# Query transposes for two heads at a time, their low parts written in the next unit, and later casts of the key weights in an encoder layer

## The chip, the cores and the metric

The kernel runs on one core of a Trainium2 chip. The metric is the device time of one execution in microseconds (us); a profile of one execution shows each engine's instructions: TensorE (PE for matmuls, PEld for the weight loads ahead of them), VectorE (DVE), ScalarE (ACT), GpSimd (POOL) and SyncE (SP), which issues most transfers.

## The reference

One encoder layer is computed for two sequences of 512 tokens and 1024 features (`x_prompt` and `x_sample`), in fp32:

```
h = rms_norm(x, ln1);  q, k, v, u, g_att, g_ssm = split(h @ w_in)
q = rms_norm(q per head of 64, q_gain);  k = rms_norm(k per head of 64, k_gain)
y_att = windowed_attention(q, k, v, sink, bias, mask)   # 16 heads, 4 key heads, blocks of 128, each block sees itself and its neighbours
y_ssm = s5_branch(u, ...)                               # bidirectional state-space scan, gelu, gated
x = x + (sigmoid(g_att) * y_att + sigmoid(g_ssm) * y_ssm) @ w_out
return x + square(relu(rms_norm(x, ln2) @ w_up)) @ w_down
```

In the attention each query block of 128 tokens meets up to three key blocks; the scores get a relative bias and a mask, a learned sink logit joins the softmax, and the weights multiply the values.

## The kernel before

Matmuls run on fp32 values split in two: a high part rounded to the engine's reduced fp32 form (F32R) and a low part, the difference between the value and its high part. A product is made of three matmuls (high by high, high by low, low by high) or, where both parts of one operand fill the two halves of the 128 partitions, of two.

The order of the work is written out by hand for TensorE, ScalarE and VectorE in the parts that the change touches (in the attention part for GpSimd too). Each engine runs its instructions in that order and stops at the first that waits. The transfers that SP issues are placed by the scheduler.

**The read-out** of the state-space branch comes first. It goes through 32 groups q of two channel groups: `turn_states` copies the states of the group after (L845 on ScalarE, or L847 on VectorE, and L848 on VectorE), `read_out` makes matmuls (L858, L860) into one of two PSUM buffers `sps`, `gelu` reads that buffer (L868 on ScalarE) and so frees it for the group after the next. Between these stand 28 items of other matmul work: 12 of the last two gates (L141) and then 16 of the keys' projection with the weights `w_k`. The weights come in pieces: `Block.piece` has SP load 512 KB into one of two buffers `c_raw` (L717), ScalarE cast it to the high part (L718), and returns the difference for the low part, which VectorE makes at the end of the group (L719). The dictionary `casts` names the group in which each piece is taken. In a group the casts stand ahead of the group's `gelu` on ScalarE. `last_cast` is the same for the last gate weights (L219, L220).

**The attention part** follows. It has 8 steps (a key head j of four query heads, and a sequence), each of four units (a query block qb of 128 tokens). Inside a unit the work of three things is interleaved:

- `Unit`, the attention of the query block: `scores(h)` for four heads (two matmuls each, L1048, stationary the query tile, moving the keys' high and low parts), `largest(h)` (L1052 on VectorE, which adds the bias and finds the negated maximum as a minimum; its second instruction reads the accumulator), `exp(h)` (L1058 on ScalarE).
- The unit before it (`prev`): `turn(i)` transposes the weights (L1064), `high(i)` and `low(i)` split them (L1068 on ScalarE, L1073 on VectorE), `value(i, part)` multiplies the values (L1080), `lower_part` copies half of the result (L1084 on ScalarE, tile `ol`) and `add` sums the halves (L1090, two instructions on VectorE). `add` runs in the unit after that.
- `Tile`, the queries of the next step: `project` (24 matmuls, L724), `square` (L1001 on ScalarE, tile `sq`), and a unit later, as `rows`: `power` (L1005 on VectorE, L1007 and L1008 on GpSimd), `norm`, `turn`, `high` and `low`.

The queries take this form. `norm` writes the normed tile (128 tokens by four heads of 64) to the first half of `qn`, and GpSimd copies it to the second, so that each head stands there twice:

```
self.qn = ap.tile([P, G, 2, HD], F32, tag="qn", name="qn")
V.tensor_mul(self.qn[:, :, 0], self.psv, self.rq[...])          # L1012
GP.tensor_copy(self.qn[:, :, 1], self.qn[:, :, 0])              # L1013
```

`turn` transposes each head with its double (four transposes, L1018), so that a head's 64 features lie in partitions 0 to 63 and again in 64 to 127. `high` writes the rounded, scaled value to all 128 partitions (one ScalarE instruction, L1023), and `low` overwrites partitions 64 to 127 with the difference (one VectorE instruction, L1027). The keys lie in both halves of the partitions too (`key_copies`, `key_turn`), so that one matmul against a query tile sums high and low part.

In a unit the order on VectorE around the change is: first minimum, `power`, `add`, second minimum, `prev.low(0)`, `norm`, third minimum, and so on; `rows.low` closes the unit. On TensorE `prev.value(0, 1)` needs `prev.low(0)`, and everything behind it follows in order. `acc` buffers (three in PSUM) hold the projections and the transposed queries.

Of the kernel before, what the change touches and what calls it, by code (L numbers as in the profile page):

```python
# [11 lines left out]
F32 = mybir.dt.float32  # L12
F32R = mybir.dt.float32r
I32 = mybir.dt.int32
AF = mybir.ActivationFunctionType
ALU = mybir.AluOpType
AX = mybir.AxisListType

P = 128
# [10 lines left out]
G = 4  # L30
HD = 64
# [32 lines left out]
def hybrid_layer(ctx, tc, x, xT, rel, onehot, early, w_qkv, w_ug, q_gain, k_gain, sink,  # L64
# [102 lines left out]
    def slot(pool):  # L167
        return [pool.tile([P, KT, HALF], F32R, tag=f"act{i}", name=f"act{i}") for i in range(2)]
# [603 lines left out]
    with tc.tile_pool(name="ssmo", bufs=2, reuse_waits="tile") as sp:  # L772
# [133 lines left out]
        casts = {0: [last_cast], 1: [last_cast], 2: [lambda: w_k.piece(0)], 3: [lambda: w_k.piece(1)], 8: [lambda: w_k.piece(2)], 9: [lambda: w_k.piece(3)],  # L906
# [46 lines left out]
    with tc.tile_pool(name="att", bufs=2, reuse_waits="tile") as ap:  # L953
# [32 lines left out]
        class Tile:  # L986
# [23 lines left out]
            def norm(self):  # L1010
                self.qn = ap.tile([P, G, 2, HD], F32, tag="qn", name="qn")
                V.tensor_mul(self.qn[:, :, 0], self.psv, self.rq[:, :, None].to_broadcast([P, G, HD]))  # L1012
                GP.tensor_copy(self.qn[:, :, 1], self.qn[:, :, 0])  # L1013

            def turn(self):
                self.pt = acc()
                for h in range(G):
                    PE.transpose(self.pt[:, h * P:(h + 1) * P], self.qn[:, h].rearrange("p a d -> p (a d)"), ident)  # L1018

            def high(self):  # L1020
                self.ptv = self.pt.rearrange("p (h t) -> p h t", h=G)
                self.dst = queries[self.key][:, :, self.t * P:(self.t + 1) * P]
                S.activation(self.dst, self.ptv, AF.Copy, scale=gain_q)  # L1023

            def low(self):
                dst = self.dst[64:128]
                V.scalar_tensor_tensor(dst, self.ptv[64:128], gain_q[64:128], dst.bitcast(F32),  # L1027
                                       op0=ALU.mult, op1=ALU.subtract)
# [164 lines left out]
        prev = owed = lower = None  # L1193
# [5 lines left out]
        if True:  # L1199
            rows = entry()  # L1200
            for i, (j, sq) in enumerate(steps):
# [8 lines left out]
                for qb in range(NB):  # L1210
# [21 lines left out]
                    cur.largest(1)  # L1232
                    if n3:
                        prev.turn(0)
                        prev.high(0)
# [56 lines left out]
                    if rows:  # L1292
                        if not sooner:
                            rows.high()
                        rows.low()
# [25 lines left out]
                if i == len(steps) - 2:  # L1321
# [3 lines left out]
                    y_tiles = [[[t_[:, 0:4, :], t_[:, 4:8, :]] for t_ in slot(slot_a)], split_slot()]  # L1325
            ahead = Column(1)
# [733 lines left out]
```

## Time and profile before

| what | value |
|---|---|
| time, median of 3 runs | 1470.08 us (1469.82 to 1471.71) |
| time of the profiled execution | 1469.22 us |
| span of the profiled execution | 1467.4 us |
| TensorE matmul busy | 1446.3 us, 99% |
| VectorE busy | 1094.6 us, 75% |
| ScalarE busy | 764.2 us, 52% |
| GpSimd busy | 168.9 us, 12% |
| granted TensorE clock | 0.999 |

The span is the time from the first to the last instruction of the profiled execution; the execution's own time is 1.8 us longer. In a row of the timeline stand the start, the duration, the engine, the line of the kernel, the operation, the tiles (written from read), the shapes, and in brackets the idle time before it and what ended it. In a row of a group stand the count, the busy time, the mean duration in ns and the idle time before. Busy time of TensorE counts matmuls whose ends are modelled and which overlap, so a wait shows first as a gap between starts.

### The profile page before, as it was taken

How to read it: one execution, taken by the hardware profiler on the slowest of the kernel's cores; microseconds unless marked ns; L12 is line 12 of the kernel's file. 1: busy time of each engine (PE TensorE's matmuls, PEld its weight loads, DVE VectorE, ACT ScalarE, POOL GpSimd, SP SyncE). 2: the span in 40 equal slices, each digit the busy share in tenths (PEclk: the TensorE clock that was granted, in tenths of full speed). 3: DMA queues.
4: the chain of work that ended last, by engine and by line, in shares of the span. 5: the costliest groups of instructions: out<-in, count | busy, mean ns of one | idle time of the engine just before them, and what ended most of it. 6: DMA issues, size and time to landing. Idle time of an engine off the chain costs nothing.

```text
span 1467.4 us, 21580 instructions
## 1 busy us (share of the span) xinstructions
PE 1446.3 (99%) x7782; PEld 1234.1 (84%) x7782; DVE 1094.6 (75%) x1836; ACT 764.2 (52%) x1366; POOL 168.9 (12%) x270
## 2 busy tenths in 40 slices
PE   6999999999999999999999999999999999999998
PEld 5888888888999899987888888888888888888887
DVE  7799979975636889888974689877776588575653
ACT  5489862233426778787532355554554444333332
POOL 4111120000223333343101000000000000000000
PEclk9999999999999999999999999999999999999999
DMA  8355567259941413236964134544443894454441
GB/s 300 112 171 174 161 206 268 101 178 290 307 131 35 121 46 89 95 130 217 303 212 144 72 115 165 174 149 147 155 158 123 302 346 147 158 177 153 129 129 58
DMA packets 129239, 243.86 MB, mean 166 GB/s; under 512 B 16060, under 2 KB 59324, under 8 KB 129133
## 3 DMA queue, kind: packets, MB, share of 16 engines
q1 hardware_dynamic: 104684, 186.87, 40.4%
q10 hardware_dynamic: 21888, 46.15, 8.3%
q0 software_dynamic: 2560, 9.48, 2.0%
q8 instruction: 61, 1.00, 0.3%
q14 instruction: 46, 0.37, 0.1%
HBM read 173.20 MB, written 81.82 MB: 174 GB/s over the span
## 4 chain that ended last, share of the span: by engine, by line
PE 91%; DVE 3%; ACT 2%; DMA 1%; issue 1%; POOL 1%; SPq 0%; DVEq 0%; ACTq 0%; POOLq 0%
PE bank L115 14%; PE bank L116 14%; PE bank L117 14%; PE acc L141 11%; PE acc L724 8%; PE acc L753 5%; PE acc L115 3%; PE acc L117 3%; PE acc L116 3%; PE po L1080 2%; PE sps L604 2%; PE sps L1048 2%; PE sps L860 2%; PE tps L1064 2%; PE lag L619 1%
## 5 line engine op out<-in xcount | busy, mean ns | idle before, releaser
L116 PE MATMUL bank<-b_lo,a_hi 128*128 128x512 f32 x440 | 171.2, 389 | 0.0
L117 PE MATMUL bank<-b_hi,a_lo 128*128 128x512 f32 x440 | 171.2, 389 | 0.0
L115 PE MATMUL bank<-b_hi,a_hi 128*128 128x512 f32 x440 | 171.2, 389 | 0.0
L724 PE MATMUL acc<-w_hi,hT 128*128 128x256 f32 x768 | 165.0, 291 | 0.0
L141 PE MATMUL acc<-hT,c_hi 128*128 128x512 f32 x512 | 161.1, 394 | 0.0
L1933 ACT CAST a_hi<-d_a 128x1024 fp32r<-128x1024 f32 x55 | 58.0, 1054 | 178.1 <-PE bank L116 175.2
L1934 DVE TENSOR_TENSOR a_lo<-d_a,a_hi 128x1024 fp32r<-128x1024 f32 x55 | 67.3, 1223 | 99.4 <-ACT a_hi L1933 97.3
L724 PEld LDWEIGHTS acc<-w_hi,hT 128*128 128x128 f32 x768 | 126.7, 190 | 1.7
L141 PEld LDWEIGHTS acc<-hT,c_hi 128*128 128x128 f32 x512 | 94.6, 188 | 21.0 <-issue 2.5
L724 PE MATMUL acc<-w_lo,hT 128*128 128x256 f32 x384 | 108.2, 282 | 0.0
L141 PE MATMUL acc<-hT,c_lo 128*128 128x512 f32 x256 | 100.3, 392 | 0.0
L115 PE MATMUL bank<-act,u_hi 128*128 128x512 f32 x256 | 99.6, 389 | 0.0
L116 PE MATMUL bank<-act,u_hi 128*128 128x512 f32 x256 | 99.6, 389 | 0.0
L117 PE MATMUL bank<-act,u_lo 128*128 128x512 f32 x256 | 99.6, 389 | 0.0
L117 PEld LDWEIGHTS bank<-b_hi,a_lo 128*128 128x128 f32 x440 | 82.6, 188 | 17.3
L115 PEld LDWEIGHTS bank<-b_hi,a_hi 128*128 128x128 f32 x440 | 82.6, 188 | 17.1
L116 PEld LDWEIGHTS bank<-b_lo,a_hi 128*128 128x128 f32 x440 | 82.6, 188 | 17.1
L1058 ACT ACTIVATE p<-p,nmx 128x257 f32<-128x257 f32 (+1 forms) x128 | 72.1, 564 | 27.0 <-DVE nmx L1052 24.3
L724 PEld LDWEIGHTS acc<-w_lo,hT 128*128 128x128 f32 x384 | 73.0, 190 | 2.5
L1052 DVE CUSTOM_DVE_ANT_0 p<-sps,bias,nsink 128x256 f32<-128x256 f32 (+1 forms) x128 | 69.2, 541 | 2.9 <-PE sps L1048 0.4
L1717 ACT CAST u_hi<-s 128x512 fp32r<-128x512 f32 x64 | 39.3, 621 | 59.8 <-PE bank L116 43.1
L1934 DVE TENSOR_TENSOR b_lo<-k,b_hi 128x1024 fp32r<-128x1024 f32 x55 | 66.9, 1217 | 0.0
(387 smaller groups left out, 3622.9 us busy)
## 6 DMA issues: line engine op xcount, KB each, us to landing
d_a<-a_scr SPq DMA_DIRECT2D x55, 512.0 KB, 3.6
u_raw<-in_w_up_dram SPq DMA_DIRECT2D x32, 512.0 KB, 5.7
a_scr<-t ACTq DMA_DIRECT2D x64, 256.0 KB, 2.1
k<-in_w_down_dram SPq DMA_DIRECT2D x32, 512.0 KB, 5.7
a_scr<-a ACTq DMA_DIRECT2D x48, 256.0 KB, 3.3
c_raw<-in_w_ug_dram SPq DMA_DIRECT2D x44, 256.0 KB, 3.6
ct_scr<-ctab SPq DMA_DIRECT2D x16, 576.0 KB, 3.3
ctab_in<-ct_scr SPq DMA_DIRECT2D x32, 288.0 KB, 4.7
```

The costliest lines, as they stand in the source:

```text
L115: PE.matmul(ps, a[0], b[0], start=first, stop=False)
L116: PE.matmul(ps, a[0], b[1], start=False, stop=False)
L117: PE.matmul(ps, a[1], b[0], start=False, stop=last)
L141: PE.matmul(self.ps[s], self.w[p == 2][:, k, :], hT[s][p == 1][:, k, :], start=i % (3 * KT) == 0, stop=i % (3 * KT) == 3 * KT - 1)
L604: PE.matmul(ps[:, i * P:(i + 1) * P], bm[:, ri, g, :], u_sb[:, g, :], start=True, stop=True)
L724: PE.matmul(ps, act[p == 2][:, k, col:col + P], self.w[k // 4][p == 1][:, k % 4, :], start=i == 0, stop=i == 3 * KT - 1)
L753: PE.matmul(self.ps[s], w_g[self.m][p == 2][:, k, :], y_part(s, int(p == 1), k), start=k + p == 0, stop=k == KT - 1 and p == 2)
L1052: V.tensor_tensor_reduce(self.p[:, h, 1:1 + self.nk], self.s[h][:, 0:self.nk], biases[self.j][h][:, b0:b0 + self.nk], -1.0, nsink[:, hh:hh ...
L1058: S.activation(p, p, AF.Exp, bias=self.nmx[:, h:h + 1], scale=-1.0, accum_out=self.sums[:, h, self.qb:self.qb + 1])
L1717: S.copy(hi, src)
L1933: S.copy(hi, src)
L1934: V.tensor_sub(lo, src, hi.bitcast(F32))
```

## The change

Three things change.

1. `norm` writes the four heads once, GpSimd's copy is gone, and `turn` transposes two heads at a time: two transposes instead of four. After them the even head of a pair lies in partitions 0 to 63 and the odd one in 64 to 127. `high` writes each to its own half of the query tile (two ScalarE instructions on 64 partitions and 256 columns instead of one on 128 and 512), and `low` writes the difference to the other half (two VectorE instructions on 64 partitions and 256 columns instead of one on 64 and 512). The odd heads' high parts so lie in partitions 64 to 127 and their low parts in 0 to 63; the keys lie in both halves.
2. `rows.low` no longer runs at the end of its unit. It is kept as `low_rows` and runs in the next unit, behind the second minimum and ahead of `prev.low(0)`.
3. The four pieces of the key weights are taken in groups 4, 6, 9 and 11 of the read-out instead of 2, 3, 8 and 9.

```diff
-        casts = {0: [last_cast], 1: [last_cast], 2: [lambda: w_k.piece(0)], 3: [lambda: w_k.piece(1)], 8: [lambda: w_k.piece(2)], 9: [lambda: w_k.piece(3)],
+        casts = {0: [last_cast], 1: [last_cast], 4: [lambda: w_k.piece(0)], 6: [lambda: w_k.piece(1)], 9: [lambda: w_k.piece(2)], 11: [lambda: w_k.piece(3)],
                  17: [lambda: w_v.piece(0)], 18: [lambda: w_v.piece(1)], 20: [lambda: w_v.piece(2)], 21: [lambda: w_v.piece(3)]}
...
             def norm(self):
-                self.qn = ap.tile([P, G, 2, HD], F32, tag="qn", name="qn")
-                V.tensor_mul(self.qn[:, :, 0], self.psv, self.rq[:, :, None].to_broadcast([P, G, HD]))
-                GP.tensor_copy(self.qn[:, :, 1], self.qn[:, :, 0])
+                self.qn = ap.tile([P, G, HD], F32, tag="qn", name="qn")
+                V.tensor_mul(self.qn, self.psv, self.rq[:, :, None].to_broadcast([P, G, HD]))
 
             def turn(self):
                 self.pt = acc()
-                for h in range(G):
-                    PE.transpose(self.pt[:, h * P:(h + 1) * P], self.qn[:, h].rearrange("p a d -> p (a d)"), ident)
+                for m in range(G // 2):
+                    PE.transpose(self.pt[:, m * P:(m + 1) * P], self.qn[:, 2 * m:2 * m + 2].rearrange("p a d -> p (a d)"), ident)
 
             def high(self):
-                self.ptv = self.pt.rearrange("p (h t) -> p h t", h=G)
-                self.dst = queries[self.key][:, :, self.t * P:(self.t + 1) * P]
-                S.activation(self.dst, self.ptv, AF.Copy, scale=gain_q)
+
+                q = queries[self.key][:, :, self.t * P:(self.t + 1) * P].rearrange("p (m e) t -> p m e t", e=2)
+                pt = self.pt[:, 0:G // 2 * P].rearrange("p (m t) -> p m t", m=G // 2)
+                self.halves = []
+                for e, (own, other) in enumerate(((slice(0, 64), slice(64, P)), (slice(64, P), slice(0, 64)))):
+                    hi, lo, src = q[own, :, e], q[other, :, e], pt[own]
+                    S.activation(hi, src, AF.Copy, scale=gain_q[own])
+                    self.halves.append((hi, lo, src, gain_q[own]))
 
             def low(self):
-                dst = self.dst[64:128]
-                V.scalar_tensor_tensor(dst, self.ptv[64:128], gain_q[64:128], dst.bitcast(F32),
-                                       op0=ALU.mult, op1=ALU.subtract)
+                for hi, lo, src, gain in self.halves:
+                    V.scalar_tensor_tensor(lo, src, gain, hi.bitcast(F32), op0=ALU.mult, op1=ALU.subtract)
...
                     cur.largest(1)
+                    if low_rows:
+                        low_rows()
+                        low_rows = None
                     if n3:
                         prev.turn(0)
                         prev.high(0)
...
                     if rows:
                         if not sooner:
                             rows.high()
-                        rows.low()
+                        low_rows = rows.low
                     project(4)
```

On VectorE, in the third unit of a step of the attention part (lines 1052, 1005, 1090, 1073 and 1027 as above; an `ISA` row is a minimum, the second one the read of its accumulator), before:

```order
L1052 ISA nmx 128x1
L1027 SCALAR_TENSOR_TENSOR qa<-acc,gain_q,qa 64x4x128
L1052 ISA p,nmx<-sps,bias,nsink 128x384
L1052 ISA nmx 128x1
L1005 TENSOR_REDUCE ms<-sq 128x4
L1090 TENSOR_TENSOR ya<-po,ol 64x2x128 x2
L1052 ISA p,nmx<-sps,bias,nsink 128x384
L1052 ISA nmx 128x1
L1073 TENSOR_TENSOR pl<-tps,ph 128x512
L1012 TENSOR_TENSOR qn<-acc,rq 128x4x64
```

And with the change, where the lines of the same instructions are 1055, 1005, 1093, 1076 and 1031:

```order
L1055 ISA nmx 128x1
L1055 ISA p,nmx<-sps,bias,nsink 128x384
L1055 ISA nmx 128x1
L1005 TENSOR_REDUCE ms<-sq 128x4
L1093 TENSOR_TENSOR ya<-po,ol 64x2x128 x2
L1055 ISA p,nmx<-sps,bias,nsink 128x384
L1055 ISA nmx 128x1
L1031 SCALAR_TENSOR_TENSOR qa<-acc,gain_q,qa 64x2x128 x2
L1076 TENSOR_TENSOR pl<-tps,ph 128x512
L1012 TENSOR_TENSOR qn<-acc,rq 128x256
```

The queries' low part moved from ahead of the unit's first minimum to between its second minimum and the low part of the weights, and became two instructions.

On ScalarE, at the start of the read-out (L868 reads a group's buffer, L845 copies states, L151 reads a gate's buffer, L872 and L154 issue stores), before:

```order
L868 ACTIVATE ysb<-sps 128x256
L872 DMA y_scr<-ysb 128x512
L718 CAST w_hi<-w_raw 128x512
L868 ACTIVATE ysb<-sps 128x256
L845 COPY st<-h 64x512
L718 CAST w_hi<-w_raw 128x512
L151 COPY sg<-acc 128x8x64
L868 ACTIVATE ysb<-sps 128x256
L872 DMA y_scr<-ysb 128x512
```

And with the change:

```order
L868 ACTIVATE ysb<-sps 128x256
L872 DMA y_scr<-ysb 128x512
L868 ACTIVATE ysb<-sps 128x256
L845 COPY st<-h 64x512
L151 COPY sg<-acc 128x8x64
L868 ACTIVATE ysb<-sps 128x256
L872 DMA y_scr<-ysb 128x512
L718 CAST w_hi<-w_raw 128x512
L868 ACTIVATE ysb<-sps 128x256
```

The first cast of the key weights moved behind the reads of two more groups and of one gate's buffer.

On SP, at the same place (L831, L833 and L835 load a group's inputs and tables), before:

```order
L717 DMA w_raw<-in_w_qkv_dram 128x512 x2
L831 DMA u_sb<-u_scr_77 128x256
L833 DMA toep<-toep_scr 128x256
L835 DMA ctab_in<-ct_scr 128x2x288
L717 DMA w_raw<-in_w_qkv_dram 128x512
L831 DMA u_sb<-u_scr_77 128x256
```

And with the change:

```order
L717 DMA w_raw<-in_w_qkv_dram 128x512
L831 DMA u_sb<-u_scr_77 128x256
L833 DMA toep<-toep_scr 128x256
L835 DMA ctab_in<-ct_scr 128x2x288
L831 DMA u_sb<-u_scr_77 128x256
L833 DMA toep<-toep_scr 128x256
L835 DMA ctab_in<-ct_scr 128x2x288
L717 DMA w_raw<-in_w_qkv_dram 128x512
```

The load of the third piece moved behind the loads of two groups.

More of the change, by code (lines that the diff above doesn't have):

```diff
@@ L1192, in hybrid_layer @@
         pending = []
-        prev = owed = lower = None
+        prev = owed = lower = low_rows = low_keys = None
         y_rows, made = [], None
@@ L1325, in hybrid_layer @@
                     y_tiles = [[[t_[:, 0:4, :], t_[:, 4:8, :]] for t_ in slot(slot_a)], split_slot()]
+            assert not low_rows and not low_keys
             ahead = Column(1)
```

## The prediction

> **What bounds the kernel now.** I read the page first, then the busy time by stretches, then the waits, then single units of the attention part by the timeline. The page's busy line:
>
> ```profile
> PE 1446.3 (99%) x7782; PEld 1234.1 (84%) x7782; DVE 1094.6 (75%) x1836; ACT 764.2 (52%) x1366; POOL 168.9 (12%) x270
> ```
>
> TensorE sets the time. But the shares are averages over stages, and the change touches two: the read-out (about 325 to 417 us) and the attention part (about 436 to 676). The stretch from 500 to 540, in the attention part (columns: length, then PE, PEld, DVE, ACT and POOL busy, each with its instructions, clock, DMA):
>
> ```profile
> 500.00:540.00 40.00, 39.94 (x296) 37.03 (x295) 35.00 (x93) 31.68 (x82) 14.82 (x26) 1.00 0.33 99
> ```
>
> Here VectorE is busy 35.00 of 40 and ScalarE 31.68, so there is little room behind TensorE. The groups of that part, and the waits of TensorE and of its weight load over the whole kernel:
>
> ```profile
> L1027 DVE SCALAR_TENSOR_TENSOR qa<-acc,gain_q,qa 64x512 fp32r<-64x512 f32 x32 | 24.2, 757 | 20.2 <-ACT qa L1023 20.0
> ...
> L1018 PE MATMUL acc<-ident,qn 128*128 128x128 f32 x128 | 19.7, 277 | 1.2 <-POOL qn L1013 1.2
> ```
>
> ```profile
> PE acc L1018 <- POOL qn L1013: 1.2, 2, 0.8
> ...
> PE sps L860 <- ACT st L845: 0.8, 1, 0.8
> PE sps L858 <- ACT ysb L868: 0.6, 1, 0.6
> ```
>
> ```profile
> PEld po L1080 <- DVE pl L1073: 3.9, 12, 0.5
> ```
>
> The reader is to see that TensorE hardly waits, and that where it waits in the attention part it is for `low(0)` (L1073), the low half of the transposed weights of the unit before, which `value(0, 1)` (L1080) takes. It waits already, if only for 3.9 us in 12 places. So what decides is how late VectorE finishes `low(0)` in each unit.
>
> A unit by its VectorE rows, the third of a step (qb = 2):
>
> ```profile
> 580.26 0.08 DVE L1052 DVE_READ_ACCUMULATOR2_ANT nmx<- 128x1 f32 x1
> 580.37 0.76 DVE L1027 SCALAR_TENSOR_TENSOR qa<-acc,gain_q,qa 64x512 fp32r<-64x512 f32 x1
> 581.16 0.62 DVE L1052 CUSTOM_DVE_ANT_0 p<-sps,bias,nsink 128x384 f32<-128x384 f32 x1
> 581.70 0.08 DVE L1052 DVE_READ_ACCUMULATOR2_ANT nmx<- 128x1 f32 x1
> 581.70 0.41 DVE L1005 TENSOR_REDUCE ms<-sq 128x4 f32<-128x256 f32 x1
> 582.03 0.84 DVE L1090 TENSOR_TENSOR ya<-po,ol 64x256 f32<-64x256 f32 x2
> 582.90 0.62 DVE L1052 CUSTOM_DVE_ANT_0 p<-sps,bias,nsink 128x384 f32<-128x384 f32 x1
> 583.45 0.08 DVE L1052 DVE_READ_ACCUMULATOR2_ANT nmx<- 128x1 f32 x1
> 583.45 0.69 DVE L1073 TENSOR_TENSOR pl<-tps,ph 128x512 fp32r<-128x512 f32 x1
> 584.05 0.41 DVE L1012 TENSOR_TENSOR qn<-acc,rq 128x256 f32<-128x256 f32 x1
> ```
>
> The queries' low part (L1027, 580.37) stands ahead of the unit's first minimum, where VectorE would mostly wait for scores anyway. From 581.16 on there is no gap. `low(0)` ends at 584.14, and TensorE takes it at 584.62:
>
> ```profile
> 584.62 0.40 PE L1080 MATMUL po<-pl,va 128*128 128x512 f32 x1
> ...
> 585.77 0.60 PE L1018 MATMUL acc<-ident,qn 128*128 128x128 f32 x4
> ```
>
> **The change, part by part.** Transposes: 128 become 64. Four start within 0.60 us and one lasts 0.277, so starts lie (0.60 - 0.277) / 3 = 0.108 us apart; TensorE saves 2 x 0.108 = 0.22 us in each of 32 tiles, **-7.0 us**. The POOL copy of qn disappears, and with it at most the 1.2 us that TensorE waited for it: **-1.0**.
>
> ScalarE's high part becomes two instructions on 64 partitions. Rows for half the elements (by form):
>
> ```profile
> L1068 ACT CAST ph<-tps 128x512 fp32r<-128x512 f32 x80 | 46.1, 576 | 2.6 <-PE tps L1064 2.0
> ...
> L1127 ACT CAST va<-acc 128x256 fp32r<-128x256 f32 x8 | 3.0, 373 | 16.9 <-PE acc L724 16.9
> ```
>
> Half a cast costs 0.373, not half of 0.576. The present instruction lasts 0.67, so a half lies between 0.37 and 0.67 - 0.20 = 0.47 us; I take 0.435, a pair of 0.87, where the next one starts 0.57 after the single one now (587.38 to 587.95 below). Everything behind it on ScalarE, `sq` and then `ol` (L1084), is 0.3 us later (0.17 to 0.37).
>
> VectorE's low part becomes two as well. Rows of the neighbours:
>
> ```profile
> L1090 DVE TENSOR_TENSOR ya<-po,ol 64x256 f32<-64x256 f32 x64 | 26.4, 412 | 0.4
> ...
> L983 DVE SCALAR_TENSOR_TENSOR kl<-tps,gain_k,kh 128x512 fp32r<-128x512 f32 x8 | 6.0, 750 | 11.1 <-ACT kh L982 11.1
> L1443 DVE SCALAR_TENSOR_TENSOR rn_xn<-x_all,rs,ln_bc 128x1024 f32<-128x1024 f32 x4 | 5.1, 1280 | 0.5 <-PE sps L1451 0.5
> ...
> L544 DVE SCALAR_TENSOR_TENSOR bk<-bb 128x128 f32<-128x128 f32 x8 | 2.4, 303 | 0.3
> ```
>
> The same operation takes 0.303 at 128 columns, 0.750 at 512 and 1.280 at 1024. Between the first two, 256 columns come to 0.303 + 0.447 / 3 = 0.45; by the slope of the last two they are 0.265 less than the 0.757 of now, 0.49. The cheapest row is the 0.412 of L1090, whose second half also reads partitions 0 to 63 and writes 64 to 127. I take 0.47. L1027 starts 0.11 after the start of the accumulator's read ahead of it (L1073 starts together with it), and the next start is 0.79 after its own where it lasts 0.76; so a block of 0.11 + 2 x (0.47 + 0.03) = **1.11 us** (0.99 with 0.412, 1.15 with 0.49). [...]
>
> The place is what matters. Before, the low part stood in the gap ahead of the first minimum. Now the block stands between the second minimum and `low(0)`, and what stands ahead of it can hardly move up: the two additions (L1090) wait for `ol`, and `ol` comes later by the ScalarE halves. In this unit:
>
> ```profile
> 580.37 0.62 ACT L1058 ACTIVATE p<-p,nmx 128x385 f32<-128x385 f32 x1 [0.16 <-DVE nmx L1052]
> ...
> 581.38 0.58 ACT L1084 COPY ol<-po 64x512 f32<-64x512 f32 x1
> ```
>
> `ol` ends at 581.96; 0.16 of the 0.3 goes into the wait of 0.16, so 582.10 now. Additions 0.87 (582.03 to 582.90), minimum 0.55, block 1.11, `low(0)` 0.69, semaphore 0.05: 585.37 for `value(0, 1)` instead of 584.62, **+0.75**. The other three units of this step:
>
> ```profile
> 569.17 0.68 DVE L1073 TENSOR_TENSOR pl<-tps,ph 128x512 fp32r<-128x512 f32 x1
> ...
> 570.33 0.40 PE L1080 MATMUL po<-pl,va 128*128 128x512 f32 x1
> ```
>
> ```profile
> 574.16 0.58 ACT L1084 COPY ol<-po 64x512 f32<-64x512 f32 x1
> ...
> 577.72 0.50 PE L1080 MATMUL po<-pl,va 128*128 128x512 f32 x1
> ```
>
> ```profile
> 587.38 0.67 ACT L1023 ACTIVATE qa<-acc,gain_q 128x512 fp32r<-128x512 f32 x1
> 587.95 0.37 ACT L1001 ACTIVATE sq<-acc 128x256 f32<-128x256 f32 x1
> 588.35 0.58 ACT L1084 COPY ol<-po 64x512 f32<-64x512 f32 x1
> ...
> 591.64 0.50 PE L1080 MATMUL po<-pl,va 128*128 128x512 f32 x1
> ```
>
> First unit: nothing ahead of `low(0)` moves up, so 569.17 + 1.11 + 0.69 + 0.05 = 571.02 against 570.33, +0.69. Second: 574.74 + 0.3 + 0.87 + 0.55 + 1.11 + 0.69 + 0.05 = 578.31 against 577.72, +0.59. Fourth, whose minimum takes 0.41 on 256 columns: 588.93 + 0.3 + 3.13 = 592.36 against 591.64, +0.72. The mean is 0.69. The block stands ahead of a `low(0)` in 28 units that also have the additions: **+19.3 us**; all that follows `value(0, 1)` on TensorE, projections, the tile's transposes and so the next high part, moves with it. Behind `low(0)` VectorE is later by as much, so `low(1)` and `low(2)` may hold TensorE too, 0 to 4 us in all: **+1**.
>
> The casts of the key weights: ScalarE waited for the first one, and TensorE for what stood behind it (0.6 + 0.8, above):
>
> ```profile
> 330.14 0.41 SPq L717 DMA_DIRECT2D w_raw<-in_w_qkv_dram  x1
> ...
> 336.10 0.62 ACT L718 CAST w_hi<-w_raw 128x512 fp32r<-128x512 f32 x1 [5.70 <-DMA w_raw<-in_w_qkv_dram]
> ```
>
> Two groups later the piece has landed, and SP's table loads no longer stand behind the third piece's wait for a free buffer. VectorE's differences move along, into gaps. The last piece is cast in group 11; the first key multiplication, 13th of 28 items spread over 32 groups, runs in group 14. **-1.4**, or 0 if the wait comes back elsewhere.
>
> Sum: 19.3 + 1.0 - 7.0 - 1.0 - 1.4 = +10.9. The profiled execution took 1469.2 us (span 1467.4), so 1480.1; the median of the runs, 1470.1, lies 0.9 higher: **1481**. With the cheap ends (ScalarE +0.17, which counts in three units of four, and a block of 0.99) a stall is 0.69 - 0.12 - 0.10 = 0.47: 28 x 0.47 - 9.4 = +3.8. With the dear ends (+0.37, 1.15) it is 0.78: 28 x 0.78 + 2 - 9.4 = +14.4. Own range of the forecast: 1474 to 1485.
>
> **The rivals.** First, TensorE's saving comes through (faster). For it: TensorE is busy 99%, VectorE loses the 20.2 us in which it waited for the high part, and with them the first minimum comes earlier. It decides from a stall of 9.4 / 28 = 0.34 us per unit downward: the block would have to cost 0.76 or `ol` come 0.35 earlier. With stalls of 0 to 0.2 us in 28 units the sum is -9.4 to -3.8, so 1460.7 to 1466.3, about 1463. Against it: the cheapest row puts two halves at 0.88 with their gaps.
>
> Second, the two cancel: a stall of 0.34 x 28 = 9.4, so 1470. That needs every half at or below its cheapest row and ScalarE no later.
>
> Third, ScalarE becomes the pace: halves of 0.47 push `ol`, the casts of `ph` and the exponentials back one behind the other, and the waits for `low(1)` and `low(2)` come out at 4 to 8 us: 28 x 0.78 + 4 to 8 - 9.4, so 1486.5 to 1490.5. For it: 31.68 of 40 busy already. Against it: ScalarE has waits to give, such as the 0.16 at 580.37.
>
> Fourth, the read-out doesn't do what it says, and the wait only moves to a later group: 1482.4 with the rest as forecast.
>
> **How the numbers follow.** A measurement of this kernel tells 0.2%, 2.9 us, from no change. Forecast, with the fourth rival in it, 0.64; third rival 0.12; both slower. First rival 0.17, faster. Second 0.07, the same. So slower 0.76, same 0.07, faster 0.17. The range reaches from 1464, in the middle of the first rival, to 1488: some 0.09 is left out below and 0.08 above.
>
> **What would show it.** In the changed profile the wait of the weight load of `value(0, 1)` for `pl` would stand at the top of TensorE's waits with some 19 us in about 28 places; VectorE would idle before the additions for `ol`, and no longer for the high part. The low halves would be 64 instructions of 0.45 to 0.49 us, the high halves 64 of 0.37 to 0.47. Around 337 us TensorE would wait for nothing. I am wrong if TensorE's wait for `pl` stays near 4 us: then the time falls by the transposes; and wrong in size if the halves run below 0.41.

## The result and the profile after

The changed kernel takes **1488.2 us** (median of 4 runs, 1486.64 to 1490.22), the kernel before beside it 1469.95 (1469.59 to 1471.71). The ratio is 1.0124, with a 95% interval of 1.0109 to 1.0139: slower by 18.3 us, where +11 was forecast. That lies above the forecast's own range (1474 to 1485) and just above its wide one (1464 to 1488). The profiled execution after took 1486.64 us, with a span of 1484.9, 17.5 us more than the span before.

The busy line of the page after:

```profile
PE 1443.6 (97%) x7718; PEld 1227.8 (83%) x7718; DVE 1106.0 (74%) x1868; ACT 774.8 (52%) x1398; POOL 154.3 (10%) x238
```

TensorE's busy time fell only from 1446.3 to 1443.6 us, and its share from 99% to 97%: it has less to do and waits more. Where it waits, and for whom, over the whole kernel (total us, times, longest), with the two waits of VectorE that moved:

```profile
PEld po L1083 <- DVE pl L1076: 34.4, 44, 1.4
PE po L1083 <- DVE pl L1076: 21.8, 37, 1.1
DVE p L1055 <- PE sps L1051: 18.6, 24, 1.1
DVE qa L1031 <- ACT qa L1026: 8.5, 3, 3.0
```

The weight load's wait for the low part of the transposed weights is 34.4 us instead of 3.9, and the matmul's own wait 21.8. It waits in 44 places, where the prediction named some 28: L1083 is the line of every product with a low part, not of `value(0, 1)` alone. VectorE waits 8.5 us for the queries' high part, where it waited 20.0. It waits 18.6 us for scores instead, so TensorE and VectorE now wait for each other in turn. The stretch from 500 to 540 shows the same for all engines:

```profile
500.00:540.00 40.00, 35.81 (x256) 32.36 (x255) 33.87 (x90) 30.34 (x78) 12.53 (x19) 1.00 0.32 96
```

TensorE is busy 35.81 of 40 where it was 39.94, and VectorE and ScalarE do not take up that time (33.87 after 35.00, 30.34 after 31.68). A waiting loop, not a new full engine, sets the pace. The new instructions by form:

```profile
L1031 DVE SCALAR_TENSOR_TENSOR qa<-acc,gain_q,qa 64x256 fp32r<-64x256 f32 x64 | 30.9, 483 | 9.9 <-ACT qa L1026 8.5
L1026 ACT ACTIVATE qa<-acc,gain_q 64x256 fp32r<-64x256 f32 x64 | 29.7, 464 | 0.5
L1017 PE MATMUL acc<-ident,qn 128*128 128x128 f32 x64 | 12.3, 273 | 0.4 <-DVE qn L1012 0.4
```

The third unit of a step, as the prediction took it apart, on VectorE and, in the last row, on TensorE. The unit's first score starts at 588.07:

```profile
588.62 0.62 DVE L1055 CUSTOM_DVE_ANT_0 p<-sps,bias,nsink 128x384 f32<-128x384 f32 x1 [0.65 <-PE sps L1051]
589.17 0.08 DVE L1055 DVE_READ_ACCUMULATOR2_ANT nmx<- 128x1 f32 x1
589.17 0.42 DVE L1005 TENSOR_REDUCE ms<-sq 128x4 f32<-128x256 f32 x1
589.77 0.85 DVE L1093 TENSOR_TENSOR ya<-po,ol 64x256 f32<-64x256 f32 x2 [0.19 <-ACT ol L1087]
590.65 0.62 DVE L1055 CUSTOM_DVE_ANT_0 p<-sps,bias,nsink 128x384 f32<-128x384 f32 x1
591.20 0.08 DVE L1055 DVE_READ_ACCUMULATOR2_ANT nmx<- 128x1 f32 x1
591.31 0.98 DVE L1031 SCALAR_TENSOR_TENSOR qa<-acc,gain_q,qa 64x256 fp32r<-64x256 f32 x2
592.33 0.69 DVE L1076 TENSOR_TENSOR pl<-tps,ph 128x512 fp32r<-128x512 f32 x1
```

```profile
593.08 0.51 PE L1083 MATMUL po<-pl,va 128*128 128x512 f32 x1 [0.67 <-DVE pl L1076]
```

Between the accumulator's read (591.20) and `low(0)` (592.33) stand 1.13 us; the forecast was 1.11. `value(0, 1)` starts 5.01 us after the unit's first score, where it started 4.18 after it before. Over the attention part this adds up. These rows are the first score matmul of the first and of the last unit, before and after:

```profile
451.36 0.28 PE L1048 MATMUL sps<-kh,qa 128*128 128x256 f32 x1
...
671.93 0.28 PE L1048 MATMUL sps<-kh,qa 128*128 128x256 f32 x1
```

```profile
448.65 0.28 PE L1051 MATMUL sps<-kh,qa 128*128 128x256 f32 x1
...
688.72 0.28 PE L1051 MATMUL sps<-kh,qa 128*128 128x256 f32 x1
```

The attention starts 2.7 us earlier (2.0 of them gained in the read-out, whose L858 starts span 87.7 us before and 85.7 after) and its last unit 16.8 us later: 19.5 us are lost in between. From the last unit's first score to the end it is 795.5 us before and 796.2 after.

### The profile page after: what moved, and what is told of

Read it like the earlier page. It is cut to its first block, busy times and chain, and to the rows that moved or that the text cites. A ratio compares the mean times of both kernels' runs of the same rounds, so it can differ in the third digit from the quotient of the medians.

```text
span 1484.9 us, 21462 instructions
## 1 busy us (share of the span) xinstructions
PE 1443.6 (97%) x7718; PEld 1227.8 (83%) x7718; DVE 1106.0 (74%) x1868; ACT 774.8 (52%) x1398; POOL 154.3 (10%) x238
## 4 chain that ended last, share of the span: by engine, by line
PE 80%; DVE 10%; ACT 5%; issue 2%; DMA 2%; POOL 1%; SPq 0%; DVEq 0%; ACTq 0%
PE bank L117 13%; PE bank L116 13%; PE bank L115 13%; PE acc L141 11%; PE acc L724 5%; PE acc L115 3%; PE acc L117 3%; PE acc L116 3%; PE acc L753 3%; DVE p L1055 2%; PE sps L604 2%; PE sps L860 2%; DVE qa L1031 2%; DVE ya L1093 2%; DVE pl L1076 1%
## 5 line engine op out<-in xcount | busy, mean ns | idle before, releaser
L1055 DVE CUSTOM_DVE_ANT_0 p<-sps,bias,nsink 128x256 f32<-128x256 f32 (+1 forms) x128 | 69.3, 542 | 19.9 <-PE sps L1051 18.6
```

The costliest lines, as they stand in the source:

```text
L1055: V.tensor_tensor_reduce(self.p[:, h, 1:1 + self.nk], self.s[h][:, 0:self.nk], biases[self.j][h][:, b0:b0 + self.nk], -1.0, nsink[:, hh:hh ...
```

## The experiments

Every comparison is with the kernel before on the same chip, whose median there was 1469.42 to 1469.97 us. "Last unit" is the start of the last unit's first score in the profiled execution, read as in the rows above; it shows what the attention gained or lost without what comes behind it. It is a reading of one execution: with the later casts the attention's first score alone starts between 448.3 and 449.7, so a difference of 1 us there says little. The expectations speak of two theories: by the order theory the place of the low part makes the loss, by the size theory the longer work of the halves does. The runs fall into four groups: the parts alone, the place of the halves, the halves one unit later, and the same without the pairs.

| kernel | median us | ratio, 95% interval | last unit, us |
|---|---|---|---|
| before | 1469.95 | | 671.93 |
| changed | 1488.2 | 1.0124 [1.0109, 1.0139] | 688.72 |
| `casts_alone` | 1468.21 | 0.9988 [0.9979, 0.9997] | 669.90 |
| `late_low_alone` | 1483.32 | 1.0096 [1.0082, 1.0110] | 684.59 |
| `low_in_place` | 1474.91 | 1.0036 [1.0023, 1.0050] | 676.72 |
| `after_casts_as_before` | 1489.1 | 1.0134 [1.0117, 1.0150] | 689.64 |
| `one_half_behind_minimum` | 1478.06 | 1.0055 [1.0039, 1.0070] | 675.72 |
| `low_behind_first_low_part` | 1485.13 | 1.0111 [1.0097, 1.0125] | 687.11 |
| `low_unit_later` | 1470.95 | 1.0009 [1.0000, 1.0018] | 665.22 |
| `low_later_bank_freed` | 1467.9 | 0.9987 [0.9978, 0.9995] | 665.16 |
| `low_later_turned` | 1466.0 | 0.9979 [0.9970, 0.9988] | 666.12 |
| `low_later_turned_last_step` | 1472.04 | 1.0014 [1.0005, 1.0023] | 669.70 |
| `low_later_turned_aside` | 1463.98 | 0.9964 [0.9949, 0.9978] | 665.73 |
| `before_form_low_later` | 1467.54 | 0.9987 [0.9978, 0.9996] | 666.94 |
| `before_form_low_later_turned` | 1467.79 | 0.9989 [0.9979, 0.9998] | 667.58 |
| `before_form_turned_aside` | 1464.72 | 0.9964 [0.9951, 0.9977] | 665.76 |

### The parts alone

The casts alone, in the kernel before:

```diff
-        casts = {..., 2: [lambda: w_k.piece(0)], 3: [lambda: w_k.piece(1)], 8: [lambda: w_k.piece(2)], 9: [lambda: w_k.piece(3)],
+        casts = {..., 4: [lambda: w_k.piece(0)], 6: [lambda: w_k.piece(1)], 9: [lambda: w_k.piece(2)], 11: [lambda: w_k.piece(3)],
```

> The kernel before with the key weights' casts in groups 4, 6, 9 and 11. If TensorE's two waits of 0.6 and 0.8 us at 337 us are all that the casts cost: 1468.6 us (-1.4). If the wait only moves to a later group: 1470.0, with a wait of the same size elsewhere before 420 us.

Measured 1468.21, 1.7 us less (the interval allows 0.4 to 3.1); forecast was 1.4.

The single low part of the kernel before, deferred behind the second minimum of the next unit, everything else as before:

```diff
                     cur.largest(1)
+                    if low_rows:
+                        low_rows()
+                        low_rows = None
...
-                        rows.low()
+                        low_rows = rows.low
```

> The kernel before, with nothing changed but the place: the one low part on 64 partitions and 512 columns runs in the next unit behind the second minimum. Order theory: a block of 0.9 us ahead of the weights' low part and nothing later on ScalarE, a stall of 0.3 to 0.5 us in 28 units: 1478 to 1484 us. Size theory: no halves, so no loss: 1468 to 1472.

Measured 1483.32, +13.4 us, in the range of the order theory. The place alone, with neither pairs nor casts, makes most of the loss.

The pairs and the casts, with the halves of the low part at the end of their own unit, where the low part stood:

```diff
-                        low_rows = rows.low
+                        rows.low()
```

> The change, but the queries' low part runs at the end of its own unit again; transposes in pairs, the halves and the later casts stay. If the place of the low part makes the loss (order theory), TensorE's wait for the weights' low part falls from 34 us to well below half of it; the two low halves still start about 0.4 us later behind two high halves and last 0.2 us longer, ahead of the first minimum, which costs 0.1 to 0.6 us in a unit: 1474 to 1482 us. If the halves' longer busy time makes it wherever they stand (size theory), it stays at 1486 to 1490.

Measured 1474.91, 13.3 us below the changed kernel and 5.0 above the kernel before. The 13.4 of the place alone and these 5.0 add up to the 18.3 of the change. Against `casts_alone` the pairs cost 6.7 us, though they take 64 transposes from TensorE. Three rows of this run's waits:

```profile
DVE qa L1031 <- ACT qa L1026: 25.2, 25, 3.0
PEld po L1083 <- DVE pl L1076: 12.4, 39, 0.5
PE sps L1051 <- DVE nmx L1055: 6.3, 14, 1.1
```

VectorE waits for the high halves again (25.2 us after 20.0 before), and the first minimum behind the low halves comes later. That minimum frees a buffer of the scores, and for it TensorE's matmuls now wait 6.3 us in 14 places, where it was 0.5 in one: about the size of the 6.7. The weight load's wait for `pl` also grows, from 3.9 to 12.4, but the matmuls themselves wait only 0.8 us for it. So the longer pairs of halves go into TensorE's waits in the old place too, by way of the score buffers.

The changed kernel with the casts where they were (the first diff backwards):

> The changed kernel with the key weights' casts at units 2, 3, 8 and 9 as in the kernel before. Moving them alone gave the kernel before 1.7 us. If the parts add up, this is 1.4 to 2.0 us slower than the changed kernel: 1489.6 to 1490.2. If the longer units of the changed kernel hide the casts, 1487.5 to 1488.7.

Measured 1489.1, between the two answers and 0.9 us over the changed kernel; the two ratios' intervals overlap, so between 1.4 and nothing this run does not decide.

### The place of the halves

One of the two halves stays behind the second minimum, the other goes to the end of that unit (two products behind the attention also exchange their accumulators, see below):

```diff
-            def low(self):
-                for hi, lo, src, gain in self.halves:
+            def low(self, which=slice(0, 2)):
+                for hi, lo, src, gain in self.halves[which]:
...
-                        low_rows()
-                        low_rows = None
+                        low_rows(slice(0, 1))
...
-                        low_rows = rows.low
+                        made_low, low_rows = low_rows, rows.low
+                        if made_low:
+                            made_low(slice(1, 2))
+                    elif low_rows:
+                        low_rows(slice(1, 2))
+                        low_rows = None
```

> The changed kernel with one of the two low halves left behind the second minimum and the other at that unit's end (and the exchange of two accumulators behind the attention). The block ahead of the first probability's low part shrinks from 1.13 to about 0.61 us. If the stall is the block's length, the delay of the second value product falls by about 0.5 us in each of 28 units and the time is 1472 to 1477, some half of the way from 1488.2 to what both halves at the end give. If any such work behind the second minimum costs the same (a wait once, not a length), 1483 to 1488. If the halves' place does not matter beyond their time on VectorE, 1486 to 1488.

The last unit starts at 675.72, 13.0 us before that of the changed kernel, close to 28 times the 0.51 us by which the block there is shorter (14.3); with both halves gone from that place (`low_unit_later`, next) it is 23.5. So the loss grows with the block's length. The time, 1478.06, lies 1 us above the expected range, since some 3 us of the gain are lost behind the attention. Leaving one half out altogether was not tried.

The two halves in the same unit, right behind `low(0)` instead of right ahead of it:

```diff
-                    if low_rows:
-                        low_rows()
-                        low_rows = None
                     if n3:
                         prev.turn(0)
...
                         prev.low(0)
+                    if low_rows:
+                        low_rows()
+                        low_rows = None
```

> The changed kernel with the same two low halves in the same unit, put right behind the first probability's low part instead of right ahead of it: two places exchanged on VectorE, and no work added or removed. If the stall comes from that part being made 1.1 us later, the waits for it go, the third minimum starts when it did, and the time falls to 1464 to 1472. If it is the halves' time on VectorE or ScalarE, 1484 to 1490. If the wait only moves on to the second and third low parts, 1474 to 1482.

Measured 1485.13: 3.1 us less by the medians, 1.9 by the ratios, whose intervals overlap. The expectation that `low(0)` alone carries the loss falls. In the same unit of the step as above, VectorE:

```profile
589.91 0.69 DVE L1076 TENSOR_TENSOR pl<-tps,ph 128x512 fp32r<-128x512 f32 x1
590.63 0.98 DVE L1031 SCALAR_TENSOR_TENSOR qa<-acc,gain_q,qa 64x256 fp32r<-64x256 f32 x2
591.64 0.42 DVE L1012 TENSOR_TENSOR qn<-acc,rq 128x256 f32<-128x256 f32 x1
591.98 0.61 DVE L1055 CUSTOM_DVE_ANT_0 p<-sps,bias,nsink 128x384 f32<-128x384 f32 x1
...
593.12 0.68 DVE L1076 TENSOR_TENSOR pl<-tps,ph 128x512 fp32r<-128x512 f32 x1
```

and TensorE's products with the low parts:

```profile
590.97 0.40 PE L1083 MATMUL po<-pl,va 128*128 128x512 f32 x1
...
593.86 0.50 PE L1083 MATMUL po<-pl,va 128*128 128x512 f32 x1 [0.60 <-DVE pl L1076]
```

`low(0)` is early now and its product does not wait. The third minimum and `low(1)` behind the block are as late as before, and the product with `low(1)` waits 0.60 here. `norm` (L1012) is late now as well, and the tile's transposes wait for it. Over the whole kernel:

```profile
PE po L1083 <- DVE pl L1076: 10.4, 28, 0.6
PE acc L1017 <- DVE qn L1012: 6.1, 15, 1.0
```

The matmuls' wait for `pl` halves, from 21.8 us, and the one for `qn` rises from 0.4 to 6.1. From the additions (588.49) on VectorE has no gap, and what TensorE takes is spread over that stretch; whatever is put into it delays the result that comes next. Moving the block past one of them hands most of the wait on. The third answer of the expectation names this; its price was too low. By its number the time lies in the range of the second answer, the halves' time on VectorE or ScalarE. That cause by itself falls with the next run, in which the same halves cost the attention nothing.

### The halves one unit later

The place without that cost is behind the following unit's last low part, where VectorE waits for scores anyway (0.65 us ahead of the first minimum in the changed kernel's unit above):

```diff
-                    if low_rows:
-                        low_rows()
-                        low_rows = None
...
                     if rows:
                         if not sooner:
                             rows.high()
-                        low_rows = rows.low
+                        made_low, low_rows = low_rows, rows.low
+                        if made_low:
+                            made_low()
+                    elif low_rows:
+                        low_rows()
+                        low_rows = None
```

> The change, but the low part runs at the end of the next unit, behind that unit's last low part of the weights (a whole unit after its high part). Order theory: nothing that TensorE takes in the unit stands behind the two halves, so the transposes' 7 us and the casts' 1.4 us come through, less what ScalarE's longer high part costs (0 to 4 us): 1461 to 1466 us. Size theory: 1480 or more.

The last unit starts at 665.22, 6.7 us before that of the kernel before, as expected. But the time is 1470.95, no gain, where 1461 to 1466 was expected. TensorE's rows show one place behind the attention that takes it back:

```profile
858.87 0.39 PE L117 MATMUL acc<-act,f 128*128 128x512 f32 x1
863.99 0.80 PE L115 MATMUL bank<-act,u_hi 128*128 128x512 f32 x1 [4.74 <-ACT u L1702]
```

The kernel before goes through this point without a pause (from 858.8 to 864 its TensorE is busy 5.20 of 5.20 us, and its first product on `bank` starts at 864.82 with no wait). `bank` is the first tile of the next stage's PSUM pool, laid over the accumulators `acc` of the stage before. In the programs as built, it lies on bank 0. In the kernel before the last product on bank 0 is one whose copy (L1693 there, L1702 here) ran long ago; with the halves a unit later, which read their accumulator longer, the three accumulators rotate in another order, and bank 0 holds the product that L1702 copies last. Two products exchange their accumulators:

```diff
-    p2 = product(ps_o.tile([P, HALF], F32, tag="po", name="p2"), first[0][1], B21)
+    p2 = product(acc(), first[0][1], B21)
...
-    p1 = product(acc(), first[1][0], B11)
+    p1 = product(ps_o.tile([P, HALF], F32, tag="po", name="p1"), first[1][0], B11)
```

> The run with the low halves at the end of the following unit came out of the attention 6.7 us ahead of the kernel before and lost 7.3 us at one place behind it: the first product of the MLP's next part waits 4.7 us for the accumulator that the copy at L1702 still reads, and its first rows are then slow. This kernel is that one with two products behind the attention exchanging their accumulators (the second product of the first pair takes one of the three rotating ones, the first product of the second pair the single one), so that the bank wanted first is read out early. If the accumulator's place in the rotation is the cause, the wait is gone and the time is 1462.5 to 1465, faster than before. If the loss comes from arriving early (a transfer or an engine that sets the pace there), it comes back elsewhere and the time stays at 1469 to 1472.

Measured 1467.9, between the two answers: some 3 of the 7 us are back. The first product no longer waits; the second does, since its bank is now the late one:

```profile
864.01 0.50 PE L115 MATMUL bank<-act,u_hi 128*128 128x512 f32 x1 [2.03 <-ACT u L1702]
```

Then the products were left alone, and the rotation was turned by one place with a tile that is only held for a while. At the attention's end:

```diff
+            turned = acc()
+            V.memset(turned[:, 0:1], 0.0)
             ahead = Column(1)
...
+            V.memset(turned[:, 0:1], 0.0)
             prev.lower_part()
```

> The low halves at the end of the following unit, with the three rotating accumulators turned by one place ahead of the last products (one accumulator held for a while by two memsets of one column), so that the MLP's first two products take the banks that they take in the kernel before. The exchange of two accumulators shortened the wait behind the attention from 4.7 to 2.0 us: the second product then waited for the copy at L1702, since its bank had become the late one. If the banks are the whole cause, no wait is left there, the 5.7 us that the run is ahead at that place reach the end, and the time is 1463 to 1465. If arriving early costs by itself, 1467 to 1470.

Measured 1466.0, again between the two answers. The wait at the banks is gone, but the held tile costs a wait of its own at the attention's end, where a column product wants an accumulator:

```profile
678.32 0.73 PE L753 MATMUL acc<-act,c_hi 128*128 128x512 f32 x2 [2.68 <-ACT gl L1353]
```

Beside it, the halves of the last step were put behind that unit's L1173, in front of which they stood:

```diff
+                    else:
+                        made_low, low_rows = low_rows, None
+                    if made_low and i < len(steps) - 1:
+                        made_low()
...
                         y_low(2 * qb + 1, y_rows[2 * qb + 1])
+                        if made_low:
+                            made_low()
```

> The run beside it, with the last step's low halves behind that unit's low part of the scan's output (L1173) instead of ahead of it, where TensorE waited 1.7 us for L1173 in one unit. 1 to 1.5 us below the run beside it: 1461.5 to 1464. If another wait takes that one's place, no difference.

Measured 1472.04, 6 us worse instead of better. I had taken the wait to be for L1173, but the row names the halves themselves, now with 2.6 us where they had 1.3:

```profile
PE acc L1180 <- DVE qa L1031: 2.6, 1, 2.6
```

So here too it is the accumulator: in the program as built, L1180's second product takes the bank of the transposes' tile, whose last reader is L1031, and the later the halves stand, the longer it waits. These 1.3 us are the smaller part of the 6. In this profile the granted clock is 0.83 from 650 to 660, behind this wait, and 0.83 again from 680 to 690, behind the one for the held tile, which by estimate, 10 us at 0.83, is some 1.7 us each; in `low_later_turned` it is 1.00 in both stretches. Finally the turn was put into column 4 of the gated read-out behind the attention, around its matmuls:

```diff
+                turned = acc() if m == 4 and s == 0 else None
+                if turned is not None:
+                    V.memset(turned[:, 0:1], 0.0)
                 col.multiply(max((s + 1) * 3 * KT - col.i, 0))
+                if turned is not None:
+                    V.memset(turned[:, 0:1], 0.0)
```

> The low halves at the end of the following unit, with the three accumulators turned by one place in the middle of the gated read-out (column 4, two memsets of one column on a buffer long free), so that no product waits for the held one. In the run with the turn at the attention's end the wait at the MLP's first products was gone, but 2.9 us went to a column product that waited for the held accumulator. If the banks alone took the gain away, 5 to 6 us ahead at the end: 1463 to 1465.5. If arriving early costs elsewhere, 1466 to 1470.

Measured **1463.98**, 0.9964 [0.9949, 0.9978]: faster than both kernels, within the range expected for the banks being the whole cause. There is no wait at the bank, and from its last unit on the run keeps 5.2 of its 6.2 us.

### The same without the pairs

The kernel before's four transposes and single copies, with the casts and the later low part of the runs above. First with the exchange of accumulators, then with the turn at the attention's end, then with the turn aside:

> The kernel before with its four transposes and one high and one low copy for each unit, the key weights' casts later as in the change, the low copy at the end of the following unit, and the same exchange of two accumulators behind the attention. Against the run beside it this leaves out only the transposing of two heads at a time and its halves. If what gains is the later place of the low copies, 1460 to 1464, no slower than the run beside it: the pairs save 0.22 us of TensorE a unit, and their halves cost VectorE and ScalarE about 0.6 us a unit. If the pairs' saving on TensorE comes through, 1466 to 1470, since 7 us of transposes come back.

> The kernel before's four transposes and single copies, with casts later, the low copy at the end of the following unit, and the accumulators turned as in the first run of these. At the attention's end it was 5.0 us ahead of the kernel before where the pairs were 6.8; with the banks in place 1465.5 to 1468, 1 to 2.5 us over the run with the pairs. If the pairs gave their 7 us on TensorE, 4 us or more over it.

> The same turn and the same later low copy and casts, with the four transposes and single copies of the kernel before. It was 1.5 to 1.8 us behind the pairs at the attention's end in two earlier runs. If the pairs are worth that much here, 1465 to 1467.5, 1 to 2.5 us over the run beside it; if nothing of it reaches the end, the same time within 0.5 us.

Measured 1467.54, 1467.79 and 1464.72, where the runs with pairs beside them took 1467.9, 1466.0 and 1463.98. The first lies in the range named for the pairs' saving coming through, but so does the run with pairs, since both still wait 2.0 us at the bank. The second is 1.8 us over the run with pairs, as expected, but the intervals overlap, and of the two profiles only its own shows a lower clock behind the held tile's wait (0.50 against 1.00, last section). In the last, cleanest comparison the ratios are equal to four digits, with intervals of 0.15% either way. From the attention's first score to the last unit's, the three profiles without pairs take 217.36, 217.84 and 217.30 us, those with pairs 216.49, 217.71 and 217.00. So at most 1 us of the 7 comes through even where the halves do not stand ahead of a low part, and none of it can be told in the time. A step's four units show why: 6.27, 7.27, 7.52 and 6.78 us with pairs, 6.49, 7.05, 7.41 and 6.95 without (by the starts of the first scores in the last two runs). In the first and fourth TensorE's 0.2 us come through; in the second a projection waits for the accumulator that the two halves still read (it starts 1.54 us after the unit's first score, 1.33 without pairs), and in the third a product waits for its low part (`pl` holds the weight load 4.9 us in 15 places from 455 to 650 with pairs, 0.4 us in 2 without).

## Why the prediction was right or wrong

**Direction and mechanism** were right. The wait for `pl` leads TensorE's waits in the attention, the block is where the prediction put it and as long (1.13 us for 1.11; from the first half's start to that of `low(0)` lie 1.02 us, 0.51 for each half of 0.483, and from the end of `low(0)` to its product 0.06, where 0.05 was taken), and its length carries the loss (`one_half_behind_minimum`, `late_low_alone`). What failed is the size of two terms of the sum: the stall per unit, through the delay of `ol`, and the later waits.

**The stall per unit** was sized at 0.69 and came out at 0.80. From the unit's first score to `value(0, 1)` the delays are 0.60, 0.74, 0.83 and 1.01 us, where 0.69, 0.59, 0.75 and 0.72 were forecast. The term that failed is the delay of `ol`. By the timeline it ends 0.29, 0.38, 0.15 and 0.53 us later in its unit, where 0.3 was taken for the second and fourth and 0.14, behind a wait, for the third (in the first it did not count). That is 0.08 of the 0.11 on average over the four units. The fourth unit, on ScalarE:

```profile
596.27 0.94 ACT L1026 ACTIVATE qa<-acc,gain_q 64x256 fp32r<-64x256 f32 x2
597.24 0.39 ACT L1001 ACTIVATE sq<-acc 128x256 f32<-128x256 f32 x1
597.65 0.58 ACT L1087 COPY ol<-po 64x512 f32<-64x512 f32 x1
```

From the first half to the next instruction are 0.97 us, 0.40 more than the 0.57 of the single copy, so the pair is at the dear end (halves of 0.464 against 0.435), and it starts later as well. In this unit the prediction also let the additions start 0.39 us sooner, since the low part ahead of them had gone; the later `ol` took most of that.

**The later waits**, +1 forecast with 0 to 4, are the term that was furthest off; no row of the prediction prices them. It took L1080's wait as that of `value(0, 1)`, though the line is that of the later products too. One of them, in the third unit, before and after:

```profile
587.38 0.40 PE L1080 MATMUL po<-ph,va 128*128 128x512 f32 x1
587.62 0.39 PE L1080 MATMUL po<-pl,va 128*128 128x512 f32 x1
```

```profile
595.73 0.40 PE L1083 MATMUL po<-ph,va 128*128 128x512 f32 x1
596.28 0.50 PE L1083 MATMUL po<-pl,va 128*128 128x512 f32 x1 [0.15 <-DVE pl L1076]
```

A later product with a low part starts 0.42 us behind its forerunner in the second unit and 0.55 in the third, 0.30 and 0.31 more than in the kernel before: 0.6 us a step, by estimate some 4 us in seven steps like this one. `low_behind_first_low_part` shows that such waits are real: there the results behind the block carry nearly all of the loss. Together the two terms give 28 x 0.11 + 3 = 6 of the 7 us by which the sum fell short. The third rival priced this case at 1486.5 to 1490.5, and the result lies there. Its reason is right in part: the ScalarE halves at 0.464 and the later waits came as it said, but ScalarE is not the pace, with 30.34 us busy in 40.

**TensorE's saving**, -7.0, is real as work: 64 transposes fewer. That it reaches the end, the first rival, is refuted more widely than the prediction had it. Even without the stall at most 1 us of it comes through, and in the old place the pairs cost 6.7 us.

**The smaller terms.** The wait of 1.2 us for the POOL copy is gone, with 0.4 for `norm` in its place. The casts were forecast at -1.4 and measured at -1.7 alone; the fourth rival, that the wait only moves, did not come true. Around 337 us TensorE waits for nothing. **VectorE's idle time** was predicted ahead of the additions, for `ol`; there it is 0.19 us in the unit shown and 4.0 in all, and 18.6 stand ahead of a minimum, for scores, because TensorE itself is late. The halves' durations, 0.483 on VectorE, lie in the predicted 0.45 to 0.49.

## What to carry to other kernels

When work is moved, look at the stretch it leaves and at the one it enters. Here it left a gap in which VectorE waited, and entered a stretch without gaps from which TensorE takes several results one after another; there half to nine tenths of what was inserted was paid (13.4 of 28 x 0.9 us in `late_low_alone`, 13.0 of 14.3 for one half), and moving it past one consumer handed most of the wait to the next (1485.13 us in `low_behind_first_low_part` after 1488.2). Ask also which buffer a moved reader holds: a later read keeps an accumulator longer, can turn the rotation of a pool, and the bill then comes where another stage's pool is laid over it (here 4.74 us at `bank` in `low_unit_later`).

## What the runs showed of the hardware that was not expected

**Behind seven pauses of TensorE, 2.0 to 2.7 us long, the granted clock was 0.50 to 0.70 four times and 1.00 three times; behind one of 5.1 us it was 0.50.** The longest first: stretches of `low_unit_later` around the pause of 5.1 us between two starts (columns as above; the clock is the third value from the end):

```profile
858.80:864.00 5.20, 0.47 (x4) 0.04 (x2) 5.11 (x10) 4.54 (x9) 0.00 (x0) 0.81 0.04 13
864.00:868.60 4.60, 4.60 (x11) 3.63 (x12) 4.52 (x8) 3.60 (x6) 0.00 (x0) 0.50 0.13 46
```

After the pause the granted clock is 0.50 for 4.6 us, with 11 matmuls where the kernel before made 22 in the same time. The run lost 7.3 us at this place, 4.9 in the pause and 2.4 in the slow matmuls. Shorter pauses, by the idle time in the row that ends them, and the granted clock in the 4 us behind:

| run | pause, us | ends at | clock behind it |
|---|---|---|---|
| `low_later_bank_freed` | 2.03 | 864.01 | 0.61 |
| `one_half_behind_minimum` | 2.04 | 874.13 | 1.00 |
| `before_form_low_later` | 2.02 | 866.55 | 1.00 |
| `low_later_turned_last_step` | 2.60 | 652.42 | 0.68 |
| `low_later_turned_last_step` | 2.68 | 683.03 | 0.70 |
| `before_form_low_later_turned` | 2.67 | 679.72 | 0.50 |
| `low_later_turned` | 2.68 | 678.32 | 1.00 |

The last two rows of the table are the wait of the same column product, one execution each:

```profile
679.70:683.70 4.00, 3.98 (x9) 3.14 (x10) 3.34 (x5) 2.51 (x4) 0.00 (x0) 0.50 0.00 0
```

```profile
678.30:682.30 4.00, 3.98 (x17) 3.28 (x18) 3.33 (x5) 2.52 (x4) 0.00 (x0) 1.00 0.01 3
```

So the length of the pause alone does not tell the clock behind it: near 2.0 us it was 0.61 once and 1.00 twice, near 2.7 us 0.50, 0.70 and 1.00. What decides between pauses of one length these runs do not show.

**Half the partitions and half the columns were not half the price on ScalarE.** The 64x256 half took 0.464 us and the 128x512 whole 0.675. At 512 columns the copy `ol` on 64 partitions took 0.58 us, and the cast `ph` on 128 also 0.58. Two halves on different partitions ran one after the other (0.94 for two).
